# A second accumulator in PSUM for gathered expert rows, and GpSimd rows in two more stages

## The chip, the cores and the metric

The kernel runs on one NeuronCore of a Trainium2 chip. The metric is the device time of one execution in microseconds (us). The engines are named as in the profile: PE is TensorE's matrix multiply and PEld its weight load, DVE is VectorE, ACT is ScalarE, POOL is GpSimd, and SP is the engine that issues most transfers.

## The reference

One decoder layer over 512 tokens of width 1024, in float32: three token mixers in parallel (forgetting attention, windowed attention, attention to a memory), merged by gates, and then a retrieval over 16384 single-neuron experts (PEER). The change lies in the second part, after the second normalization:

```python
def peer_ffn(h, w_q, keys1, keys2, u, v):
    q = (h @ w_q).reshape(B, S, PEER_HEADS, 2, half)
    s1 = einsum('bshd,hkd->bshk', q[..., 0, :], keys1)
    s2 = einsum('bshd,hkd->bshk', q[..., 1, :], keys2)
    v1, i1 = top_k(s1, 16); v2, i2 = top_k(s2, 16)
    cand = (v1[..., :, None] + v2[..., None, :]).reshape(B, S, PEER_HEADS, 256)
    sv, si = top_k(cand, 16)
    experts = i1[si // 16] * 128 + i2[si % 16]
    gates = softmax(sv, axis=-1)
    # per token, over its 8 heads x 16 = 128 experts e:
    a = einsum('cd,ced->ce', h_c, u[e_c])
    act = gelu(a) * g_c
    out = einsum('ce,ced->cd', act, v[e_c])
```

The layer's result is the mixers' output plus `out`.

## The kernel before, in words

The 512 tokens are four blocks of 128. Block 0 goes through the mixers and the search first, blocks 1 to 3 follow together (`GROUPS`). The experts of the four blocks are then used in two ways.

**Blocks 0 and 1 gather rows.** For each of a token's 128 experts a row of `peer_u` or `peer_v` (128 tokens x 1024 numbers, 0.5 MB) is fetched by an indirect DMA, which GpSimd issues (L836). There are 512 such rows, in this order: the u rows of block 0, the v rows of block 0, the u rows of block 1, the v rows of block 1 (`JOBS`). `step()` takes the next one. It first issues gathers up to `ahead` rows in front, into a ring of five buffers (`ROWS_IN`), from the choices to near the end of spreading with two more from the `raw` buffers. Then it uses its own row. A u row is multiplied with the normalized tokens `h2n[b]` and summed along the row by one VectorE instruction (L846), which leaves one column of `acts[b]`. A v row is scaled with its column and added to the running sum `x1[b]` in SBUF by one VectorE instruction (L855). With `apart=True` a v row is instead scaled by ScalarE (L851) and added to the same sum by GpSimd (L852). After the last u row of a block, `acts[b]` goes through Gelu and is multiplied by the gates.

**Blocks 2 and 3 are dense** (`DENSE`). For each of the 128 key blocks k, `dense_u(k)` multiplies all 128 experts' u rows with the 256 tokens on PE and applies Gelu into `ga(k)`, a ring of 58 slots in the two tiles `soon` and `late`. The result is multiplied with the gates, which are zero except for chosen experts, and `dense_v(k)` multiplies it with the v rows into four PSUM banks. `dense_v` and some of `dense_u` work in pairs of rounded numbers, high part and remainder: ScalarE casts the high part, VectorE subtracts it from the original, and PE runs three products (`mm3`). A plain `dense_u` uses full float32 matmuls instead. `split_u(k)` says which form a tile takes: before, the first 57 tiles and then every second one are plain.

The stages, in order of time:

1. The mixers of block 0, then those of blocks 1 to 3, with the search and the first rows of block 0 beside them (`beside`), 190 rows in all (`EARLY_ROWS`).
2. The second search, of blocks 1 to 3, on VectorE, with `step(apart=True)` beside it and the first eight `dense_u`.
3. Choosing: `choose` for blocks 2 and 3 and `numbers_of` for block 1, on VectorE, while PE computes 24 plain `dense_u`. A row is taken for each unit of cost (`AMONG`).
4. Spreading: for 64 batches of four tokens, `build_sides` makes one-hot matrices on VectorE (L1031) and scales them on ScalarE (L1034). `spread` multiplies them on PE into a PSUM bank (L1046). VectorE multiplies part of that bank into `soon` (L1049), and ScalarE copies the rest out in three pieces (L1052), from where it goes to a DRAM buffer `gd`. 25 plain `dense_u` are laced in, and 0.8 rows for each batch (`STEPS_N`).
5. The final loop over k = 0 to 127: for each k, the gate product (L1091), the casts (L1094, L1096) and remainders (L129, L1099) of `dense_v(k+1)`, the rows that are due, the start of one `dense_u`, then PE's work of `dense_v(k)`. The rows that are left are spread evenly over the loop.

From stage 3 on, the order of instructions on PE, VectorE and GpSimd is the order of the program; ScalarE's and SP's is set by the framework's scheduler. PSUM has eight banks, which `bank(tag)` hands out: `mm` two, `tp` two, `sc` two, `tg` and `acc` one each. In spreading, `tg` holds the numbers 0 to 127 that L1031 compares with, `acc` the transposed choices, and the spread tiles alternate between `sc` and `tp`.

Of the kernel before, what the change touches and what calls it, by code (L numbers as in the profile page):

```python
# [21 lines left out]
NK = 128  # L22
# [15 lines left out]
U_SPLIT = 2  # L38
# [5 lines left out]
SPARE, STEPS_N = 4, 0.8  # L44
# [3 lines left out]
TG = 32  # L48
# [5 lines left out]
EARLY_ROWS, PER_ROW = 190, 4.6  # L54
# [3 lines left out]
def tile_block(ctx: ExitStack, tc: tile.TileContext, t: dict, out: bass.AP):  # L58
# [765 lines left out]
    known, issued, done, ahead, flying, rpool = [2 * NJ], [0], [0], [AHEAD], {}, []  # L824

    def step(apart=False):
# [16 lines left out]
        if tab == "u":  # L843
            scr = big.tile([128, D], BF16, tag="junk", name="scr")
            tc.keep_in_program_order(
                V.scalar_tensor_tensor(scr, r, 1.0, h2n[b], op0=OP.mult, op1=OP.mult, accum_out=acts[b][:, c]))  # L846
            if j == NJ - 1:
                A.activation(acts[b], acts[b], AF.Gelu)
                V.tensor_mul(acts[b], acts[b], gate[b])
        elif apart:  # L850
            A.activation(r, r, AF.Copy, scale=acts[b][:, c])  # L851
            G.tensor_tensor(x1[b], x1[b], r, op=OP.add)  # L852
        else:
            tc.keep_in_program_order(
                V.scalar_tensor_tensor(x1[b], r, acts[b][:, c], x1[b], op0=OP.mult, op1=OP.add))  # L855
# [57 lines left out]
    side[0] = iter(())  # L913
    for lb, b in enumerate(GROUPS[1]):
        x1[b] = xb[:, lb]
# [9 lines left out]
    def ga(k):  # L925
        s = k % (LAG + 1)
        return soon[:, s] if s <= LAG - GA_LATE else late[0][:, s - (LAG + 1 - GA_LATE)]
# [23 lines left out]
    def split_u(k):  # L951
        return k >= LAG and (k - LAG) % U_SPLIT > 0

    def dense_u(k):
# [4 lines left out]
        if split_u(k):  # L959
            hi, lo = (gp[0].tile([128, D], F32R, tag=tag, name=tag, bufs=1) for tag in ("uhi", "ulo"))  # L960
# [19 lines left out]
    h2f = chunks(dp.tile([128, KC, TD], F32, name="h2f", bufs=1))  # L980
# [28 lines left out]
    numbers = bank("tg")[:, :NK]  # L1009
# [3 lines left out]
    def turn_block(i):  # L1013

        ps = bank("acc")
# [21 lines left out]
    def spread(n):  # L1037
# [6 lines left out]
        ps = bank(("sc", "tp")[n % 2]).rearrange("p (t k) -> p t k", t=4)  # L1044
# [36 lines left out]
    def operands(k):  # L1081
# [6 lines left out]
        if k >= KEPT:  # L1088
            m = gq[k - k % GK][:, :, k % GK]
            g = a.rearrange("p (g t) -> p g t", t=TG)  # L1090
            V.tensor_mul(g, m, g)  # L1091
# [30 lines left out]
    credit[0] = 0.0  # L1122
# [171 lines left out]
```

## Time and profile before

| | us |
|---|---|
| median of 3 runs | 1597.82 (1595.21 to 1600.01) |
| the profiled execution | 1602.33 |
| its span, first to last instruction | 1600.5 |
| PE busy | 1532.0 |
| VectorE busy | 1404.6 |
| ScalarE busy | 788.1 |
| GpSimd busy | 798.4 |

Busy times are unions of an engine's instructions, so overlapping ones count once. A row of a group gives an instruction's line, engine, operation, output and inputs, shapes and count; behind the first bar stand the busy time in us and the mean duration of one in ns, behind the second the idle time of the engine just ahead of them and what ended it. A line of the timeline gives start, duration and instruction; `xN` merges N of them. Instructions that follow one another on an engine overlap a little, so the distance from start to start is shorter than the duration.

### The profile page before, as it was taken

To read this page: it belongs to the slowest core of one execution; us is meant where nothing else is said; L and a number is where in the kernel's file an instruction comes from. 1 tells how busy PE (TensorE), PEld (TensorE's weight loads), DVE (VectorE), ACT (ScalarE), POOL (GpSimd) and SP (SyncE) were. 2 spreads that over 40 slices of the span, in tenths; PEclk is the share of its full clock that TensorE was granted. 3 is DMA by queue.
4 is the path that set the end of the run, shared out by engine and by line. 5 is a ranking of instruction groups with operands and counts; after the bars stand their busy time and mean duration, and the time that the engine had idled before them with its cause. 6 is when DMAs were issued, how large, how long until landed. Compare 5 with 4: busy or idle time off the path is not lost.

```text
span 1600.5 us, 26571 instructions
## 1 busy us (share of the span) xinstructions
PE 1532.0 (96%) x9142; PEld 1384.7 (87%) x9142; DVE 1404.6 (88%) x2722; ACT 788.1 (49%) x1776; POOL 798.4 (50%) x624
## 2 busy tenths in 40 slices
PE   6999999999998989998898999999999999999998
PEld 5999899898897989898787999788888888888887
DVE  5677477989998999999899999888889999989997
ACT  6787426656445433454214888544444444443442
POOL 1100015776666456568764333465555565565561
PEclk9999999999998999999999999999999999999999
DMA  8586656898998799994798999999999999999995
GB/s 303 181 280 221 234 198 218 293 372 313 333 354 307 264 353 338 366 348 145 257 392 318 353 369 346 363 409 398 391 398 408 407 406 410 410 391 409 411 407 219
DMA packets 178358, 531.86 MB, mean 332 GB/s; under 512 B 17456, under 2 KB 46384, under 8 KB 178224
## 3 DMA queue, kind: packets, MB, share of 16 engines
q0 software_dynamic: 73728, 268.47, 44.7%
q1 hardware_dynamic: 94704, 226.04, 38.9%
q10 hardware_dynamic: 9792, 35.66, 5.6%
q8 instruction: 72, 1.18, 0.3%
q14 instruction: 62, 0.51, 0.1%
HBM read 515.42 MB, written 14.68 MB: 331 GB/s over the span
## 4 chain that ended last, share of the span: by engine, by line
PE 65%; DVE 12%; DMA 11%; issue 7%; ACT 3%; POOL 3%; SPq 0%; DVEq 0%; POOLq 0%; ACTq 0%
PE mm L974 16%; PE mm L144 7%; PE mm L143 7%; PE mm L145 7%; DMA row<-in_peer_v_dram,eidx 5%; DMA row<-in_peer_u_dram,eidx 4%; PE sc L144 3%; PE sc L145 3%; PE tp L143 3%; PE tp L145 3%; PE tp L144 3%; PE sc L143 3%; DVE wlo L129 2%; POOL row L836 2%; DVE mg L855 2%
## 5 line engine op out<-in xcount | busy, mean ns | idle before, releaser
L836 POOL DMA_INDIRECT row<-in_peer_v_dram,eidx x256 | 359.7, 1405 | 263.0 <-DVE mg L855 170.6
L836 POOL DMA_INDIRECT row<-in_peer_u_dram,eidx x256 | 335.0, 1308 | 271.4 <-DVE scr L846 117.6
L846 DVE SCALAR_TENSOR_TENSOR scr<-row,own 128x1024 bf16<-128x1024 f32 x256 | 312.6, 1221 | 31.6 <-DMA row<-in_peer_u_dram,eidx 29.9
L129 DVE TENSOR_TENSOR wlo<-raw,whi 128x1024 fp32r<-128x1024 f32 (+1 forms) x244 | 304.6, 1250 | 33.9 <-ACT whi L117 31.6
L855 DVE SCALAR_TENSOR_TENSOR mg<-row,acts,mg 128x1024 f32<-128x1024 f32 x237 | 304.2, 1283 | 21.0 <-DMA row<-in_peer_v_dram,eidx 18.7
L974 PE MATMUL mm<-h2f,hhi 128*128 128x256 f32 x944 | 217.4, 381 | 1.1 <-ACT late L976 1.1
L117 ACT CAST whi<-raw 128x1024 fp32r<-128x1024 f32 (+1 forms) x148 | 154.9, 1049 | 103.9 <-PE mm L144 69.9
L974 PEld LDWEIGHTS mm<-h2f,hhi 128*128 128x128 f32 x944 | 177.5, 191 | 25.7 <-ACT late L976 1.5
L190 POOL TENSOR_TENSOR rsy<-rsv,mhalf 128x4 f32<-128x4 f32 (+5 forms) x25 | 39.9, 1600 | 191.9 <-DVE rsv L189 117.6
L1094 ACT CAST ah<-ga 128x256 fp32r<-128x256 f32 x116 | 47.1, 408 | 144.3 <-PE tp L144 110.1
L143 PE MATMUL mm<-hhi,whi 128*128 128x384 f32 x320 | 111.2, 348 | 1.6 <-DVE mg L642 1.0
L145 PE MATMUL mm<-hhi,wlo 128*128 128x384 f32 x320 | 111.0, 347 | 0.0
L144 PE MATMUL mm<-hlo,whi 128*128 128x384 f32 x320 | 111.0, 347 | 0.0
L1096 ACT CAST whi<-raw 128x1024 fp32r<-128x1024 f32 x96 | 100.4, 1047 | 20.8 <-PE tp L145 9.9
L976 ACT ACTIVATE ga<-mm 128x256 f32<-128x256 f32 x84 | 32.5, 388 | 158.8 <-PE mm L974 158.5
L143 PE MATMUL sc<-whi,ah 128*128 128x512 f32 x256 | 107.2, 419 | 0.0
L143 PE MATMUL mm<-whi,hhi 128*128 128x256 f32 (+1 forms) x360 | 104.6, 292 | 1.6 <-DVE mg L642 1.0
L144 PE MATMUL mm<-wlo,hhi 128*128 128x256 f32 (+1 forms) x360 | 103.9, 289 | 2.2 <-DVE wlo L129 2.2
L145 PE MATMUL mm<-whi,hlo 128*128 128x256 f32 (+1 forms) x360 | 103.2, 288 | 0.5 <-DVE hlo L631 0.5
L144 PE MATMUL sc<-wlo,ah 128*128 128x512 f32 x256 | 101.1, 395 | 2.4 <-DVE wlo L129 2.4
L143 PE MATMUL tp<-whi,ah 128*128 128x512 f32 x256 | 101.1, 395 | 0.0
L145 PE MATMUL sc<-whi,al 128*128 128x512 f32 x256 | 101.0, 394 | 0.0
(286 smaller groups left out, 3950.3 us busy)
## 6 DMA issues: line engine op xcount, KB each, us to landing
raw<-in_peer_v_dram SPq DMA_DIRECT2D x96, 512.0 KB, 7.8
hhi<-in_uT_dram ACTq DMA_DIRECT2D x68, 512.0 KB, 7.8
raw<-in_w_tr_dram SPq DMA_DIRECT2D x48, 512.0 KB, 5.2
raw<-in_w_nat_dram SPq DMA_DIRECT2D x40, 512.0 KB, 5.9
last<-in_peer_v_dram SPq DMA_DIRECT2D x32, 512.0 KB, 7.0
hhi<-in_uT_dram SPq DMA_DIRECT2D x26, 512.0 KB, 7.1
raw<-in_w_o_dram SPq DMA_DIRECT2D x24, 512.0 KB, 5.6
gd<-st SPq DMA_DIRECT2D x24, 512.0 KB, 12.0
```

The source lines that it names most:

```text
L117: A.copy(hi[:, :n * w], raw[:, :n * w])
L129: V.tensor_sub(lo, raw, hi.bitcast(F32))
L143: PE.matmul(ps, lh, rh, start=first, stop=False)
L144: PE.matmul(ps, lh, rl, start=False, stop=False)
L145: PE.matmul(ps, ll, rh, start=False, stop=last)
L190: G.tensor_tensor(y, v, mhalf[:, :n], op=OP.pow)
L836: G.indirect_dma_start(out=r, out_offset=None, in_=t["peer_" + tab], in_offset=bass.IndirectOffsetOnAxis(ap=eidx[b][:, j:j + 1], axis=0))
L846: V.scalar_tensor_tensor(scr, r, 1.0, h2n[b], op0=OP.mult, op1=OP.mult, accum_out=acts[b][:, c]))
L855: V.scalar_tensor_tensor(x1[b], r, acts[b][:, c], x1[b], op0=OP.mult, op1=OP.add))
L974: PE.matmul(ps[:, :TD], w[:, dc], h2f[dc], start=dc == 0, stop=dc == KC - 1)
L1094: A.copy(ah, a)
L1096: A.copy(hi, raw)
```

## The change

- A tile `two` of two PSUM banks takes the place of the banks `tg` and `acc`, which are its halves in the mixers. In spreading, `numbers` and `turned` use the two `tp` banks, and the spread tiles use the two `sc` banks alone.
- After the second search (`vacant`), the v rows that VectorE takes are summed in `two`, and that sum is added to `x1[b]` after the block's last row. GpSimd's rows go on to `x1[b]` in SBUF. For the u rows of block 1, ScalarE copies `h2n[1]` to `two`, and VectorE reads it there.
- A u row can be taken apart: GpSimd multiplies it, ScalarE sums it.
- Among the choices, rows are taken in pairs on VectorE, and after every second pair one more is scaled by ScalarE. GpSimd adds it ahead of the next pair (`beside_vector`), released by a one-column copy on VectorE.
- In spreading, 0.95 rows are taken for each batch, and those with a job number divisible by four are taken apart. Before the second search 183 rows are taken, not 190.
- In the final loop the gate product is made for four k at once (in two pieces where the ring wraps from one tile to the other). All `dense_u` from the 59th on are split, with a second pair of buffers for high part and remainder in the place of `h2f`, and the last of them come one k earlier.

```diff
-U_SPLIT = 2
-SPARE, STEPS_N = 4, 0.8
+SPARE, STEPS_N = 4, 0.95
-EARLY_ROWS, PER_ROW = 190, 4.6
+EARLY_ROWS, PER_ROW = 183, 4.6
...
-    BANKS = {"mm": 2, "tg": 1, "tp": 2, "sc": 2, "acc": 1}
+    BANKS = {"mm": 2, "tp": 2, "sc": 2}
+    two = psum.tile([128, D], F32, name="two", bufs=1)
     def bank(tag):
+        if tag not in BANKS:
+            return two[:, :512] if tag == "tg" else two[:, 512:]
...
+    begun_v, scaled, vacant = set(), [], [False]
+    def beside_vector():
+        while scaled:
+            b, r = scaled.pop(0)
+            V.tensor_copy(r[:, 0:1], r[:, 0:1])
+            G.tensor_tensor(x1[b], x1[b], r, op=OP.add)
-    def step(apart=False):
+    def step(apart=False, later=False):
...
-        if tab == "u":
+        if tab == "u" and b and j == 0:
+            A.copy(two, h2n[b])
+        if tab == "u" and apart:
+            G.tensor_tensor(r, r, h2n[b], op=OP.mult)
+            A.activation(r, r, AF.Copy, accum_out=acts[b][:, c])
+        elif tab == "u":
             scr = big.tile([128, D], BF16, tag="junk", name="scr")
             tc.keep_in_program_order(
-                V.scalar_tensor_tensor(scr, r, 1.0, h2n[b], op0=OP.mult, op1=OP.mult, accum_out=acts[b][:, c]))
+                V.scalar_tensor_tensor(scr, r, 1.0, two if b else h2n[b], op0=OP.mult, op1=OP.mult,
+                                       accum_out=acts[b][:, c]))
...
+        elif apart:
+            A.activation(r, r, AF.Copy, scale=acts[b][:, c])
+            if later:
+                scaled.append((b, r))
+            else:
+                G.tensor_tensor(x1[b], x1[b], r, op=OP.add)
+        elif not vacant[0]:
...
+        elif b not in begun_v:
+            begun_v.add(b)
+            tc.keep_in_program_order(V.tensor_scalar(two, r, acts[b][:, c], None, op0=OP.mult))
+        else:
+            tc.keep_in_program_order(
+                V.scalar_tensor_tensor(two, r, acts[b][:, c], two, op0=OP.mult, op1=OP.add))
+        if j == NJ - 1:
...
+            else:
+                beside_vector()
+                V.tensor_add(x1[b], x1[b], two)
...
     def split_u(k):
-        return k >= LAG and (k - LAG) % U_SPLIT > 0
+        return k > LAG
...
-            hi, lo = (gp[0].tile([128, D], F32R, tag=tag, name=tag, bufs=1) for tag in ("uhi", "ulo"))
+            if k % 2:
+                hi, lo = (gp[0].tile([128, D], F32R, tag=tag, name=tag, bufs=1) for tag in ("uhi", "ulo"))
+            else:
+                hi, lo = halves_u[0][:, 0], halves_u[0][:, 1]
...
-    numbers = bank("tg")[:, :NK]
+    numbers = bank("tp")[:, :NK]
+    turned = bank("tp")
-        ps = bank("acc")
+        ps = turned
-        ps = bank(("sc", "tp")[n % 2]).rearrange("p (t k) -> p t k", t=4)
+        ps = bank("sc").rearrange("p (t k) -> p t k", t=4)
...
-        if k >= KEPT:
-            m = gq[k - k % GK][:, :, k % GK]
-            g = a.rearrange("p (g t) -> p g t", t=TG)
-            V.tensor_mul(g, m, g)
+        if k >= KEPT and k % GK == 0:
+            i = 0
+            while i < GK:
+                run = ga_run(k + i, GK - i)
+                n = run.shape[1]
+                g = run.rearrange("p k (g t) -> p k g t", t=TG)
+                V.tensor_mul(g, gq[k][:, :, i:i + n].rearrange("p g k t -> p k g t"), g)
+                i += n
...
-            while credit[0] >= AMONG and done[0] < known[0]:
-                credit[0] -= AMONG
+            while credit[0] >= 2.0 * AMONG and done[0] < known[0] - 3:
+                credit[0] -= 2.0 * AMONG
+                pairs += 1
+                beside_vector()
                 step()
+                step()
+                if pairs % 2:
+                    step(apart=True, later=True)
+    beside_vector()
...
-            step()
+            step(apart=done[0] % 4 == 0)
...
-        while k_u < min(NK, LAG + (NK - LAG) * (k + 1) // (NK - 5)):
+        while k_u < min(NK, LAG + (NK - LAG) * (k + 1) // (NK - 6)):
```

More of the change, by code (lines that the diff above doesn't have):

```diff
@@ L842, in step @@
         r, c = flying.pop(n), slice(j, j + 1)
-        if tab == "u":
+        if tab == "u" and b and j == 0:
[4 more added lines that the diff above has]
+        elif tab == "u":
             scr = big.tile([128, D], BF16, tag="junk", name="scr")
             tc.keep_in_program_order(
-                V.scalar_tensor_tensor(scr, r, 1.0, h2n[b], op0=OP.mult, op1=OP.mult, accum_out=acts[b][:, c]))
-            if j == NJ - 1:
+                V.scalar_tensor_tensor(scr, r, 1.0, two if b else h2n[b], op0=OP.mult, op1=OP.mult,
[8 more added lines that the diff above has]
+            tc.keep_in_program_order(
+                V.scalar_tensor_tensor(x1[b], r, acts[b][:, c], x1[b], op0=OP.mult, op1=OP.add))
+        elif b not in begun_v:
+            begun_v.add(b)
+            tc.keep_in_program_order(V.tensor_scalar(two, r, acts[b][:, c], None, op0=OP.mult))
+        else:
+            tc.keep_in_program_order(
+                V.scalar_tensor_tensor(two, r, acts[b][:, c], two, op0=OP.mult, op1=OP.add))
+        if j == NJ - 1:
+            if tab == "u":
                 A.activation(acts[b], acts[b], AF.Gelu)
                 V.tensor_mul(acts[b], acts[b], gate[b])
[L850 to L855, printed above, removed]
+            else:
+                beside_vector()
+                V.tensor_add(x1[b], x1[b], two)
     def beside():
@@ L925, in ga, with ga_run @@
     def ga(k):
-        s = k % (LAG + 1)
-        return soon[:, s] if s <= LAG - GA_LATE else late[0][:, s - (LAG + 1 - GA_LATE)]
+        return ga_run(k, 1)[:, 0]
+    def ga_run(k, n):
+        s, edge = k % (LAG + 1), LAG + 1 - GA_LATE
+        return soon[:, s:min(s + n, edge)] if s < edge else late[0][:, s - edge:min(s - edge + n, GA_LATE)]
     def fetch_u(k):
@@ L979, in tile_block @@
     h2T = [chunks(x) for x in pair(BIG)]
-    h2f = chunks(dp.tile([128, KC, TD], F32, name="h2f", bufs=1))
+    h2f = chunks(dp.tile([128, KC, TD], F32, tag="h2f", name="h2f", bufs=1))
+    halves_u = []
     k_u, share[0] = 0, 0.0
@@ L1121, in tile_block @@
     ahead[0] = AHEAD + MORE
-    credit[0] = 0.0
+    credit[0], pairs = 0.0, 0
     for job in (*(choose(cp, f, lb, iota_k, chosen[DENSE[lb - 1]]) for lb in (1, 2)), numbers_of(cp, f, 0, 1, iota_k)):
@@ L1177, in tile_block @@
         split(h2s[0][dc], h2s[1][dc], h2f[dc])
+    halves_u.append(dp.tile([128, 2, D], F32R, tag="h2f", name="u2", bufs=1))
     begun = []
@@ L1185, in tile_block @@
         begun = []
-        while k_u < min(NK, LAG + (NK - LAG) * (k + 1) // (NK - 5)):
-            assert not begun and not (split_u(k_u) and any(split_u(n) for _, n in us))
+        while k_u < min(NK, LAG + (NK - LAG) * (k + 1) // (NK - 6)):
+            assert not begun
             begun.append((dense_u(k_u), k_u))
             next(begun[-1][0])
-            if split_u(k_u):
-                next(begun[-1][0])
+            next(begun[-1][0])
             k_u += 1
```

2 lines of the change are left out of this document (added).

## The prediction

> **What bounds the kernel now.** I read the page first, then busy time by stage, then the groups, the waits and the timeline of the longest stage.
>
> ```profile
> span 1600.5 us, 26571 instructions
> PE 1532.0 (96%) x9142; PEld 1384.7 (87%) x9142; DVE 1404.6 (88%) x2722; ACT 788.1 (49%) x1776; POOL 798.4 (50%) x624
> ```
>
> The profiled execution took 1602.3 us, 4.5 above the median of 1597.8; the sum below is made on its span and its difference laid on the median. At 96% and 88%, PE and VectorE must be compared stage by stage:
>
> ```profile
> core 0: us, PE busy (x) PEld busy (x) DVE busy (x) ACT busy (x) POOL busy (x), PEclk, DMA share, GB/s
> 550.00:692.00 142.00, 131.32 (x836) 127.91 (x835) 134.19 (x214) 54.51 (x97) 81.54 (x67) 0.95 0.97 356
> 692.00:778.00 86.00, 78.77 (x421) 73.72 (x420) 81.20 (x507) 39.79 (x58) 70.62 (x63) 0.96 0.65 225
> 778.00:862.00 84.00, 77.68 (x361) 67.82 (x359) 80.38 (x128) 12.74 (x30) 54.05 (x41) 1.00 0.95 359
> 862.00:1016.00 154.00, 150.66 (x934) 138.72 (x935) 147.96 (x224) 128.61 (x488) 50.66 (x50) 0.98 0.97 343
> 1016.00:1600.00 584.00, 576.99 (x2934) 494.74 (x2932) 528.76 (x701) 233.53 (x357) 325.99 (x211) 1.00 0.99 390
> ```
>
> The stages are: end of the mixers and start of the second search; the rest of that search; choosing; spreading; the final loop over 128 key blocks. The reader is to see four different limits. In the search VectorE leads. In choosing and spreading both engines are within 7 us of the stage. In the final loop PE is busy for 577 of 584 us and VectorE is idle for 55. DMA is almost saturated there too (share 0.99).
>
> **The change, part by part.** Rows are 512 jobs. Before: 190 by the end of the mixers, 19 during the search, 36 among the choices (their costs sum to 36.1), 51 in spreading (64 x 0.8), so 216 in the final loop. After: 183, 19, 45 (18 pairs of VectorE rows, with a GpSimd row behind every other pair), 60 (64 x 0.95, of which 15 have a job number divisible by four and go to ScalarE and GpSimd), so 205 in the final loop. VectorE loses 7, 0, 6 and 11 rows in these places.
>
> *Fewer early rows.*
>
> ```profile
> 550.00:692.00 142.00, 74.60 (x58) 0.95 0.97 356
> 699.01 3.70 DVE L129 TENSOR_TENSOR wlo<-raw,whi 128x1024 fp32r<-128x1024 f32 x1
> L129 DVE TENSOR_TENSOR wlo<-raw,whi 128x1024 fp32r<-128x1024 f32 x95 | 115.9, 1220 | 1.8 <-ACT whi L1096 1.8
> L852 POOL TENSOR_TENSOR mg<-mg,row 128x1024 f32<-128x1024 f32 x19 | 45.2, 2379 | 0.3
> L836 POOL DMA_INDIRECT row<-in_peer_v_dram,eidx x256 | 359.7, 1405 | 263.0 <-DVE mg L855 170.6 <-issue 20.5 <-DVE scr L846 16.9
> ```
>
> The first row is the v rows of L855 alone: 58 in 74.6 us, 1.29 each, up to the point where the first GpSimd rows begin. VectorE is the fuller engine on both sides of it, so 7 x 1.29 = 9.0 us go from the path. The 19 GpSimd rows begin that much earlier, so they don't hold the end. The chain may pass through row transfers at places, so I take -8, between -10 and 0.
>
> *Choosing.* VectorE keeps 36 rows. Nine tiny copies are added, nine GpSimd adds of 2.38 us and nine ScalarE scalings (ScalarE is busy for 13 of 84). A split on VectorE beside such adds took 3.70 us instead of its usual 1.22, so an add that is late for the two sheltered rows can hold up a later operation with two SBUF inputs. Ends: 0, and 9 x 2.4 = 21 us. With VectorE at 80.4 of 84 some slack exists, and two rows of 1.28 cover an add that starts in time; I take +2, near the sheltered end. Each add waits for the tiny copy, and the next gathers' descriptors are queued on POOL behind it. POOL goes from 54 to 54 + 9 x 2.38 + 9 x 1.41 = 88 us if descriptors stay as long as they are, so it is full, and rows may come late; that is the unsheltered end.
>
> *Spreading.*
>
> ```profile
> L1034 ACT ACTIVATE o<-o,eT 128x128 f32<-128x128 f32 x256 | 81.6, 393 | 20.4 <-DVE o L1031 20.3
> L851 ACT ACTIVATE row<-row,acts 128x1024 f32<-128x1024 f32 x19 | 21.6, 1150 | 23.6 <-DMA row<-in_peer_v_dram,eidx 23.6
> 921.05 1.05 PE L1046 MATMUL sc<-o 128*128 128x128 f32 x8
> 923.72 0.60 ACT L1052 COPY st<-sc 128x128 f32<-128x128 f32 x3
> 925.76 1.05 PE L1046 MATMUL sc<-o 128*128 128x128 f32 x8
> ```
>
> PE keeps all its work (150.7 of 154), so VectorE's six fewer rows give nothing. ScalarE takes 15 x 1.15 + about 1 for the copy of the normalized rows into PSUM: 128.6 + 18 = 147. The spread tiles have two banks instead of four, so the bank written at 921.05 must be free at 925.76; ScalarE lets go of it at 924.32, a margin of 1.4 us that one 1.15 us row nearly eats. An in-order ScalarE that waits for a GpSimd product also delays PE. Ends: -2 (PE's gaps) and +10 (each of the 15 rows holding PE for some 0.7 us); I take +2, since the margin covers one row.
>
> *Final loop, PE.* 35 plain u tiles become split tiles. The first row here is a stretch in the middle of the loop, in the columns of the stages.
>
> ```profile
> 1300.00:1400.00 100.00, 100.00 (x521) 86.39 (x520) 94.43 (x112) 40.96 (x64) 59.55 (x39) 1.00 1.03 410
> 1039.75 3.45 PE mm L974 x16
> 1301.66 0.28 PE L143 MATMUL mm<-hlo,uhi 128*128 128x256 f32 x1
> 1304.48 0.40 PE L143 MATMUL sc<-whi,ah 128*128 128x512 f32 x1
> ```
>
> A plain tile occupies PE for 3.45 us; a split one, from its first matmul to the next tile's, 2.82. 35 x 0.63 = 22 us less: PE needs 555.
>
> *Final loop, VectorE.*
>
> ```profile
> L855 DVE SCALAR_TENSOR_TENSOR mg<-row,acts,mg 128x1024 f32<-128x1024 f32 x128 | 164.1, 1282 | 15.1 <-DMA row<-in_peer_v_dram,eidx 13.7
> L846 DVE SCALAR_TENSOR_TENSOR scr<-row,own 128x1024 bf16<-128x1024 f32 x88 | 107.6, 1222 | 10.0 <-DMA row<-in_peer_u_dram,eidx 8.9
> L963 DVE TENSOR_TENSOR ulo<-hhi,uhi 128x1024 fp32r<-128x1024 f32 x35 | 42.7, 1220 | 0.0
> 1429.15 1.22 DVE L963 TENSOR_TENSOR ulo<-hhi,uhi 128x1024 fp32r<-128x1024 f32 x1
> 1430.28 1.22 DVE L129 TENSOR_TENSOR wlo<-last,whi 128x1024 fp32r<-128x1024 f32 x1
> 1431.42 0.42 DVE L1099 TENSOR_TENSOR al<-ga,ah 128x256 fp32r<-128x256 f32 x1
> 1431.75 0.42 DVE L1091 TENSOR_TENSOR ga<-gq,ga 128x256 f32<-128x256 f32 x1
> 1432.09 2.60 DVE L855 SCALAR_TENSOR_TENSOR mg<-row,acts,mg 128x1024 f32<-128x1024 f32 x2
> ```
>
> From start to start a split's remainder takes 1.13 and a gate product 0.34. 35 more remainders cost +39.6. The 96 gate products (32.6) become 22 of four blocks and 4 of two, where the ring of 58 slots wraps: 22 x 1.13 + 4 x 0.60 (between 0.34 and 1.13 by size) = 27.3, so -5.3. Eleven fewer u rows: -13.4. One more add of the PSUM sum: +1.2. VectorE needs 528.8 + 22.1 = 551. ScalarE gets 35 casts more on 234 of 584 us; they are hidden by its idle time. The gathers lose 11 of 0.5 MB, about 6 of the 228 MB that 390 GB/s make in 584 us, so DMA at the 410 GB/s of the stretch 1300 to 1400 would need 541.
>
> ```profile
> DVE al L1099 <- ACT ah L1094: 17.6, 16, 3.2
> DVE mg L855 <- DMA row<-in_peer_v_dram,eidx: 13.7, 19, 2.1
> DVE scr L846 <- DMA row<-in_peer_u_dram,eidx: 8.9, 9, 2.2
> DVE wlo L129 <- ACT whi L1096: 5.6, 7, 1.6
> ```
>
> So PE (555) and VectorE (551) become equal bounds. VectorE's waits for ScalarE (17.6 + 5.6) come from a ScalarE that follows PE, and should mostly go as PE gets slack; of the 22.6 for row transfers I keep some 17, and 5 for the ends. 551 + 22 = 573, that is -11. Ends: 559 (555 and PE's own gaps of 4) and 606 (VectorE with all its idle time, 551 + 55).
>
> *PSUM as operand.* A row now reads and writes PSUM on VectorE.
>
> ```profile
> L1031 DVE TENSOR_TENSOR o<-tg,eT 128x1024 f32<-128x1024 f32 x64 | 77.7, 1217 | 0.0
> L1010 DVE COPY tg<-cst x1: 292/292/292, 511.6 to 511.6; 128x128 f32<-128x128 f32 x1
> L778 DVE CAST p<-pos 128x128 f32<-128x128 uint32 x3 | 0.7, 220 | 0.0
> ```
>
> Reading PSUM costs nothing: L1031 takes 1217 ns beside 1220 for L963 in SBUF. For writing there is one copy, 292 ns, beside 220 for a cast within SBUF. Ends: 0 and +72 ns a row. I take 0, since the in-place sum is nearer to L1031 in kind and size.
>
> [...]
>
> **Sum.** -8 + 2 + 2 - 11 = -15: span 1585.5, its execution 1587.3, median 1582.8.
>
> **The rivals.**
> - *VectorE becomes the bound and keeps its waits* (slower). In the final loop its 551 plus idle time sets the end. With all 55 the loop takes 606, +22, and the kernel is at +18, 1616; with 45, 1606. It decides once more than 37 us of idle time stay (551 + 37 = 588, which uses up the 4 us net gain elsewhere). For it: the row waits are the transfers' and DMA stays nearly full. Against: in the stretch 1300 to 1400 VectorE was 94% busy though PE set the pace, and in spreading 96%. Chance 0.17.
> - *Writing PSUM is dearer.* 72 ns on 205 rows is +14.8 in the final loop, and about +3 on the 36 + 45 before it: 1601. For it only the small copy, against it L1031. [...] Chance 0.10.
> - *Spreading pays for two banks and a full ScalarE*: +10 instead of +2, 1591. Chance 0.10.
> - *The early rows weren't on the path*: 0 instead of -8, 1591. Against it are the 134 busy of 142 us. Chance 0.09.
>
> **How the numbers follow.** The forecast has 0.54, with 1572 to 1592 as its own range. The low end of the whole range is all good ends but the choices': -10 + 2 - 2 - 25 would be 1563; as they hardly come together I stop at 1568. The high end is the first rival with 45 us of idle time and a little more, 1608. What a measurement tells from no change is 0.3%, 4.8 us. Faster: 0.54, and some 0.11 from the two rivals that end at 1591: 0.65. Slower: 0.17, and 0.03 from the PSUM price: 0.20. Same: 0.15.
>
> **What would show it.** After: the first GpSimd rows of the search some 9 us earlier; GpSimd adds in the choices beside VectorE rows at 1.28, with no split or comparison far above its usual time; the spread stage within 152 to 158 us and ScalarE above 90% of it; in the final loop 70 remainders, no plain tile but one, PE near 97% and VectorE near 96%, the wait for `ah` below 8 us. I would be wrong if rows in PSUM took 1.35, if PE stood idle in the final loop for VectorE by more than 30 us, or if POOL's adds made rows late in the choices.

## The result, and the profile after

The changed kernel takes 1615.2 us (median of six executions, 1606.8 to 1619.6) against 1598.2 for the kernel before on the same chip: a ratio of 1.0092, with a 95% interval of 1.0072 to 1.0112. On another chip it was 1612.8 against 1601.7, 1.0085 (1.0062 to 1.0107). The forecast was 1583: wrong in sign, by 32 us.

The profiled execution of the changed kernel took 1606.8 us, the shortest of its six. The first fence has the busy line of its page, the second its busy time by stage, in the columns that the prediction showed (PE, PE's weight loads, VectorE, ScalarE, GpSimd, granted clock, DMA share, GB/s). The five stretches run up to its own landmarks: the mixers of blocks 1 to 3, the rest of the second search, choosing, spreading, the final loop.

```profile
PE 1514.0 (94%) x9422; PEld 1374.8 (86%) x9422; DVE 1428.6 (89%) x2661; ACT 843.1 (53%) x1849; POOL 800.2 (50%) x648
```

```profile
427.00:655.00 228.00, 211.69 (x1344) 195.62 (x1343) 210.83 (x326) 99.07 (x219) 135.70 (x105) 0.96 0.91 325
655.00:781.00 126.00, 110.67 (x631) 105.84 (x632) 115.21 (x568) 58.71 (x90) 84.55 (x74) 0.93 0.66 235
781.00:880.00 99.00, 90.07 (x409) 78.00 (x407) 89.35 (x175) 22.39 (x40) 67.27 (x54) 0.98 0.88 334
880.00:1034.00 154.00, 148.91 (x926) 136.32 (x927) 141.97 (x215) 138.88 (x515) 93.78 (x77) 0.98 1.01 368
1034.00:1600.00 566.00, 558.19 (x3220) 488.13 (x3219) 548.32 (x645) 269.19 (x394) 271.79 (x200) 1.00 1.00 393
```

And the same kind of answer for the kernel before, at the landmarks that it has for the first three of these stretches:

```profile
427.00:645.00 218.00, 204.66 (x1320) 193.09 (x1318) 201.50 (x314) 95.33 (x205) 126.62 (x98) 0.96 0.91 325
645.00:773.00 128.00, 118.26 (x657) 112.92 (x657) 122.85 (x596) 59.10 (x93) 90.64 (x83) 0.95 0.77 281
773.00:862.00 89.00, 82.68 (x384) 72.22 (x382) 84.11 (x153) 13.16 (x30) 58.60 (x45) 1.00 0.93 347
```

Both kernels reach 427 us together. Then the mixers take 228 instead of 218 us and choosing 99 instead of 89; the rest of the search, which should have become 9 us shorter, takes 126 instead of 128, with PE busy for only 110.7 of them. Spreading is nearly as before. Only the final loop gains: 14 us by the landmarks below (the stretches of 584 and 566 both end at 1600, and so hold different tails behind the loop). So the losses in the mixers and the search, which the prediction had costed at nothing, and in choosing, which it had costed at 2, swallow the gain.

To compare kernels I use four landmarks, each the start of the first or last of a group of instructions: the last candidate sum on GpSimd (the search ends), the first comparison for the spread tiles (choosing ends), the first remainder `al` (spreading ends), the last `al<-ga` (end of the loop). These are the groups in the changed kernel:

```profile
L693 POOL TENSOR_TENSOR cand<-v x64: 201/228/1318, 201.2 to 780.9; 128x24 f32<-128x24 f32 x16, 128x16 f32<-128x16 f32 x16, 128x48 f32<-128x48 f32 x16, 128x8 f32<-128x8 f32 x8
L1069 DVE TENSOR_TENSOR o<-tp,eT x64: 1206/1214/1218, 880.7 to 1021.7; 128x1024 f32<-128x1024 f32 x64
L1142 DVE TENSOR_TENSOR al<-ga,ah x116: 409/417/427, 1033.9 to 1595.8; 128x256 fp32r<-128x256 f32 x116
```

This gives 780.9 for the end of the search, then 99.8 for choosing, 153.2 for spreading and 561.9 for the loop. All profiles by these landmarks, in us, with the ratio of the times to the kernel before on the same chip:

| kernel | search ends | choosing | spreading | loop | ratio (95%) |
|---|---|---|---|---|---|
| before | 773.2 | 89.3 | 152.7 | 575.9 | 1 |
| changed | 780.9 | 99.8 | 153.2 | 561.9 | 1.0092 (1.0072 to 1.0112) |
| changed, again | 781.1 | 98.2 | 154.0 | 563.3 | 1.0085 (1.0062 to 1.0107) |
| early183 | 761.8 | 90.1 | 148.4 | 581.4 | 0.9959 (0.9943 to 0.9974) |
| final_only | 768.6 | 89.2 | 153.1 | 571.6 | 0.9968 (0.9954 to 0.9982) |
| two_tile | 783.5 | 89.9 | 152.0 | 579.2 | 1.0093 (1.0078 to 1.0107) |
| two_tp | 772.9 | 89.9 | 150.4 | 580.3 | 1.0056 (1.0036 to 1.0075) |
| tp_only | 770.8 | 89.9 | 148.4 | 579.5 | 1.0008 (0.9991 to 1.0026) |
| sep_banks | 762.6 | 100.4 | 160.3 | 563.2 | 0.9933 (0.9919 to 0.9946) |
| sep_again | 764.8 | 97.8 | 154.7 | 563.1 | 0.9944 (0.9924 to 0.9963) |
| sep_nochoose | 760.8 | 91.0 | 155.7 | 575.2 | 0.9984 (0.9970 to 0.9999) |
| sep_noadd | 765.0 | 95.7 | 158.4 | 563.3 | 0.9935 (0.9910 to 0.9961) |
| sep_third | 763.5 | 103.1 | 155.0 | 563.1 | 0.9987 (0.9972 to 1.0003) |
| sep_spread | 756.6 | 98.4 | 152.3 | 574.3 | 0.9986 (0.9974 to 0.9997) |
| sep_more3 | 769.3 | 99.0 | 154.4 | 570.8 | 0.9961 (0.9942 to 0.9980) |
| after_tp | 768.3 | 99.2 | 160.9 | 560.9 | 0.9984 (0.9971 to 0.9997) |

Executions of one kernel differ by a few us in where the search ends (the seven profiles whose names begin with sep_ share the code of that part: 756.6 to 769.3), so one profile's landmark there counts for some 6 us either way. The boundary between spreading and the loop moves too: before, early183, tp_only and final_only share the code of spreading, and it takes 148.4 to 153.1. So the ratios decide.

### The profile page after: what moved, and what is told of

Read it like the earlier page. It is cut to its first block, busy times and chain, and to the rows that moved or that the text cites. A ratio compares the mean times of both kernels' runs of the same rounds, so it can differ in the third digit from the quotient of the medians.

```text
span 1605.0 us, 27116 instructions
## 1 busy us (share of the span) xinstructions
PE 1514.0 (94%) x9422; PEld 1374.8 (86%) x9422; DVE 1428.6 (89%) x2661; ACT 843.1 (53%) x1849; POOL 800.2 (50%) x648
## 4 chain that ended last, share of the span: by engine, by line
PE 58%; DVE 14%; issue 11%; DMA 7%; POOL 6%; ACT 3%; SPq 0%; POOLq 0%; DVEq 0%; ACTq 0%
PE mm L146 9%; PE mm L145 9%; PE mm L147 9%; PE mm L1010 5%; POOL row L846 5%; DMA row<-in_peer_v_dram,eidx 3%; PE sc L1084 3%; DVE wlo L131 3%; PE sc L146 2%; PE sc L147 2%; PE tp L146 2%; PE tp L145 2%; PE sc L145 2%; PE tp L147 2%; DVE two L877 2%
## 5 line engine op out<-in xcount | busy, mean ns | idle before, releaser
L846 POOL DMA_INDIRECT row<-in_peer_v_dram,eidx x256 | 323.4, 1263 | 276.6 <-DVE two L877 148.8
L846 POOL DMA_INDIRECT row<-in_peer_u_dram,eidx x256 | 313.4, 1224 | 239.3 <-DVE scr L861 134.6
L131 DVE TENSOR_TENSOR wlo<-raw,whi 128x1024 fp32r<-128x1024 f32 (+1 forms) x244 | 313.4, 1285 | 38.7 <-ACT whi L119 34.1
L877 DVE SCALAR_TENSOR_TENSOR two<-row,acts,two 128x1024 f32<-128x1024 f32 x169 | 217.0, 1284 | 6.1 <-DMA row<-in_peer_v_dram,eidx 3.8
L119 ACT CAST whi<-raw 128x1024 fp32r<-128x1024 f32 (+1 forms) x148 | 155.0, 1049 | 112.8 <-PE mm L146 65.3
L861 DVE SCALAR_TENSOR_TENSOR scr<-row,own 128x1024 bf16<-128x1024 f32 x128 | 156.5, 1222 | 19.9 <-DMA row<-in_peer_u_dram,eidx 19.1
L861 DVE SCALAR_TENSOR_TENSOR scr<-row,two 128x1024 bf16<-128x1024 f32 x115 | 139.5, 1213 | 2.2 <-DMA row<-in_peer_u_dram,eidx 1.3
L145 PE MATMUL sc<-whi,ah 128*128 128x512 f32 x256 | 100.8, 394 | 0.0
L146 PE MATMUL tp<-wlo,ah 128*128 128x512 f32 x256 | 100.6, 393 | 0.0
L147 PE MATMUL tp<-whi,al 128*128 128x512 f32 x256 | 100.2, 391 | 0.0
```

What stands on the lines that cost most here:

```text
L119: A.copy(hi[:, :n * w], raw[:, :n * w])
L131: V.tensor_sub(lo, raw, hi.bitcast(F32))
L145: PE.matmul(ps, lh, rh, start=first, stop=False)
L146: PE.matmul(ps, lh, rl, start=False, stop=False)
L147: PE.matmul(ps, ll, rh, start=False, stop=last)
L846: G.indirect_dma_start(out=r, out_offset=None, in_=t["peer_" + tab], in_offset=bass.IndirectOffsetOnAxis(ap=eidx[b][:, j:j + 1], axis=0))
```

## The experiments

**One part at a time, on both sides.** Theory one: the tile of two banks, which replaces the separate banks `tg` and `acc` already in the mixers, costs the 8.5 us there. Theory two: the seven early rows fewer do it. Theory three: the granted clock.

early183 is one constant of the kernel before:

```
-EARLY_ROWS, PER_ROW = 190, 4.6
+EARLY_ROWS, PER_ROW = 183, 4.6
```

> The kernel before with 183 instead of 190 rows among the mixers and nothing else; the seven rows go to later stages. The prediction's step says 8 us less up to the end of the second search, of which the final loop gives back at most 9 (seven rows of 1.28): 1590 to 1599, with the last rows of that stretch some 8 us earlier. Theory one (the shared tile of the two PSUM banks costs the mixers 8.5 us, and the seven rows were never on the path): mixers and search as before, 1598 to 1602. Theory two (the seven rows fewer are themselves what shifted the mixers and lengthened them): the mixers of blocks 1 to 3 end 8 to 9 us later, 1606.

1594.2 against 1601.0. The search ends at 761.8, against 773.2, 768.6 and 770.8 in the three profiles with 190 rows and separate banks (before, final_only, tp_only): about 9 us earlier, as the prediction's step said. The loop gets longer by 5.5, but spreading is 4.3 shorter; together they take 1.2 more. Theory two falls.

two_tile takes only the bank layout:

```
-    BANKS = {"mm": 2, "tg": 1, "tp": 2, "sc": 2, "acc": 1}
+    BANKS = {"mm": 2, "tp": 2, "sc": 2}
+    two = psum.tile([128, D], F32, name="two", bufs=1)
     def bank(tag):
+        if tag not in BANKS:
+            return two[:, :512] if tag == "tg" else two[:, 512:]
...
-    numbers = bank("tg")[:, :NK]
+    numbers = bank("tp")[:, :NK]
+    turned = bank("tp")
...
-        ps = bank(("sc", "tp")[n % 2])...
+        ps = bank("sc")...
```

> The kernel before with the two banks tg and acc made halves of one PSUM tile, the spread tiles in two banks instead of four and the table of key numbers moved; rows, choices and final loop as before. Theory one (the shared tile makes the mixers wait): mixers of blocks 1 to 3 end some 8.5 us later and spreading pays about 2, 1607 to 1610, and the order of instructions there is that of the changed kernel. Theory two (the number of early rows) and theory three (a lower granted clock by chance): mixers as before, 1598 to 1602.

1615.8: theory one, and more than it asked for. This part alone makes the kernel as slow as the whole change does. The search ends 10 to 15 us later, while spreading with two banks instead of four takes 152.0 instead of 152.7 us.

The timeline of PE shows what changes. First the kernel before, where the window attention's last block runs (line 354 transposes the probabilities, 513 accumulates in `acc`, 347 transposes the next heads' queries through `tg`):

```profile
500.21 0.49 PE L347 MATMUL tg<-cst,qn 128*128 128x128 f32 x3
500.53 1.00 PE L513 MATMUL acc<-sv,pT 128*128 128x64 f32 x8
...
505.57 1.97 PE L513 MATMUL acc<-sv,pT 128*128 128x64 f32 x8 [0.68 <-ACT pT L356]
509.25 1.65 PE L347 MATMUL tg<-cst,qn 128*128 128x128 f32 x3 [1.71 <-ACT qn L333]
```

The same work in two_tile, where `tg` and `acc` are halves of `two` (lines 350 and 516, the division on VectorE is line 374):

```profile
518.60 1.97 PE L516 MATMUL two<-sv,pT 128*128 128x64 f32 x8 [0.73 <-ACT pT L359]
523.41 1.12 PE L378 MATMUL tp<-cst,o 128*128 128x128 f32 x4 [2.83 <-DVE o L374]
524.32 0.85 PE L350 MATMUL two<-cst,qn 128*128 128x128 f32 x3
...
526.24 0.84 PE L350 MATMUL two<-cst,qn 128*128 128x128 f32 x3
```

In the kernel before a transpose into `tg` stands among the accumulations, and PE has other work while a block is finished. With the shared tile there is no transpose into the first half until the accumulators in the second are complete and divided, and PE stands idle for 2.83 us until that division (`o`) ends. The whole trace bears this out: 108 matmuls write `tg` or, in its place, the first half of `two`. In the kernel before 20 of them lie between the first accumulation of a block and its division (19 in sep_banks, below), in two_tile and in the changed kernel none. So the program's order of instructions itself is another one: what uses the two halves has been put one after the other.

The 2.83 us are only a part of the loss. From 427.5 us, where the forgetting attention's branch ends, to the first sum of the mixers' output at 611.6, the kernel before takes 184.1 us, with PE busy for 172.2; two_tile takes 194.8, from 428.6 to 623.4, with PE busy for 180.2. So 2.7 of these 10.7 us are idle time of PE, and 8.0 are work: 28 more matmuls lie in this stretch, where the window attention has been pushed back.

**The banks separated again.** sep_banks is the changed kernel with the two banks in a PSUM pool of their own, closed after the mixers:

```
-    two = psum.tile([128, D], F32, name="two", bufs=1)
+    mixing = ExitStack()
+    pair_of = mixing.enter_context(tc.tile_pool(name="mixing", bufs=1, space=PSUM))
     # tg and acc are tiles of pair_of
...
     pre.close()
+    mixing.close()
+    two = ctx.enter_context(tc.tile_pool(name="sum", bufs=1, space=PSUM)).tile([128, D], F32, ...)
```

> The changed kernel, but tg and acc are two tiles of a PSUM pool of their own, closed after the mixers; the two-bank sum is allocated from the freed banks afterwards. Theory one: the 8.5 us of the mixers come back, 1607, with the choices as slow as in the changed kernel (91 us). Theory two or three: 1615, mixers ending as late as in the changed kernel.

1590.8 against 1601.0: 24 us less than the changed kernel, three times what theory one asked for, and faster than the kernel before. Theories two and three, which asked for 1615, fall. The search ends at 762.6 instead of 781; choosing stays at 100.

Of these 18 us, 11 lie in the mixers, which end at 643.5 instead of 654.6. The other 7 lie in the rest of the search, and there the changed kernel has one wait that no other has. The fence shows ScalarE and, in its last row, PE in the changed kernel:

```profile
722.96 1.15 ACT L864 ACTIVATE row<-row,acts 128x1024 f32<-128x1024 f32 x1 [4.18 <-DMA row<-in_peer_v_dram,eidx]
731.23 1.15 ACT L864 ACTIVATE row<-row,acts 128x1024 f32<-128x1024 f32 x1 [6.48 <-DMA row<-in_peer_v_dram,eidx]
739.53 1.15 ACT L864 ACTIVATE row<-row,acts 128x1024 f32<-128x1024 f32 x1 [7.16 <-DMA row<-in_peer_v_dram,eidx]
741.52 0.47 ACT L721 COPY qp<-mm 128x384 f32<-128x384 f32 x1
742.04 1.65 PE L725 MATMUL sc<-keys,qp 128*128 128x128 f32 x6 [13.10 <-ACT qp L721]
```

ScalarE scales three rows for GpSimd, each of which it has to wait for, ahead of a copy (`qp`) that PE needs. PE stands for 13.1 us. In the other three profiles of the changed kernel this wait is 12.6, 12.7 and 12.9 us; in every other kernel, sep_banks included, the longest wait for such a copy is 2.4 to 6.9. So in the changed kernel the shared tile costs more than in two_tile because it also comes with another order in the search. Why the scheduler chose it wasn't traced.

The kernel with separate banks was timed once more on another chip:

> The kernel with separate mixer banks once more, on another chip and with more executions: 0.990 to 0.995 of the kernel before if the first comparison holds (1590.8 against 1601.0).

1591.4 against 1599.8, ratio 0.9944: it holds. This is the version that beats both kernels.

**What in the shared tile costs.** two_tp is two_tile, tp_only the kernel before, after_tp the changed kernel, each with this edit; in tp_only nothing is shared and `tg` stands unused in the mixers:

```
-            ps = bank(("tg", "tp")[n % 2])      # heads' transposes
+            ps = bank("tp")
```

> The kernel before with the shared tile of two banks, but the heads' transposes use the two tp banks alone, so that in the mixers nothing but the accumulators of attention stands in the shared tile (its second half). Theory one (a transpose into one half waits for the accumulators in the other): mixers of blocks 1 to 3 end as in the kernel before or within 3 us, 1600 to 1604. If it isn't the two halves but the tile's place or kind that costs: as with the shared tile, 1613 to 1616.

> The kernel before, in which the heads' transposes use the two tp banks alone; tg stands unused in the mixers, the accumulators keep a bank of their own, nothing is shared. If the 7 us that remained with the shared tile and transposes in tp alone come from the transposes having one bank less, this kernel is as slow, mixers of blocks 1 to 3 ending 6 to 8 us late: 1603 to 1606. If they come from accumulators in the shared tile, it is as the kernel before: 1597 to 1600.

> The changed kernel, with the shared tile kept, but the heads' transposes in the two tp banks alone. If it is transposes and accumulators in the two halves of one tile that wait for each other, the search ends some 10 us earlier than in the changed kernel (781) and the whole takes 1600 to 1605. If the tile itself costs, whatever is written into it, 1611 to 1616.

two_tp took 1604.9 (1.0056) and after_tp 1596.8 (0.9984): with the heads' transposes out of the shared tile, 0.4% of the 0.9% come back in the kernel before, and 1.0% of the some 1.5% (1.0092 or 1.0085 against 0.9933 or 0.9944) in the changed one. tp_only took 1602.5 against 1601.7: a bank less for the transposes costs nothing that can be measured, though the mixers end 6 us later, since the rest of the search is that much shorter. So most of the loss is the meeting of transposes and accumulators in one tile; after_tp gets back more than was expected of it (1600 to 1605). Some 0.4 to 0.5% remain in two_tp and after_tp, with nothing but accumulators in the shared tile during attention; their profiles show no single place for it, and it stays open.

**The final loop alone.** final_only is the kernel before with all u tiles after the ring split, the halves in the place of `h2f`, merged gate products and u one block earlier (that part of the diff, unchanged).

> The kernel before with the changed final loop alone: all u tiles after the ring are split, halves in the place of h2f, gate products for four blocks at once, u tiles done one block earlier. 216 rows stay in the loop instead of 205, summed in SBUF. The prediction's step: VectorE 551 + 11 x 1.28 = 565 busy. If VectorE's work and its 21 us of idle time set the end, the loop takes 585 and the kernel is as before, 1595 to 1600. If PE sets it (558 busy), the loop takes 570 as in the changed kernel: 1583. Mixers, search, choices and spreading as before under either.

1595.9 against 1601.0; by the landmarks the loop goes from 575.9 to 571.6 with 216 rows, and is 561.9 in the changed kernel with 205. That is nearer to the first case (no change) than to the second (562 by the landmarks). Here is the loop's busy time in final_only:

```profile
1011.00:1583.00 572.00, 555.97 (x3202) 485.15 (x3201) 559.29 (x664) 268.35 (x395) 354.31 (x211) 1.00 1.01 397
```

The next two fences have the same for the changed kernel's first profile, and for another of its profiles (after_l3), in which TensorE was granted 0.95 of its clock through the whole loop:

```profile
1034.00:1596.00 562.00, 554.19 (x3202) 484.86 (x3201) 547.11 (x643) 269.19 (x394) 271.79 (x200) 1.00 1.00 396
```

```profile
1044.00:1606.00 562.00, 553.40 (x3198) 483.83 (x3197) 546.76 (x641) 268.65 (x393) 272.53 (x200) 0.95 1.00 396
```

Between final_only and the changed kernel eleven rows leave the loop. PE's work stays (3202 matmuls, 556 and 554 us), VectorE's falls by 12.2 us, and the loop by 9.7. Nine rows make 10.7 us of VectorE's work and 12.1 of the loop between sep_nochoose and sep_again. So with 214 or 216 rows the loop follows VectorE's work. With 205 rows PE has 8 us of idle time and VectorE 15: they are nearly equal bounds, as the prediction said, and nothing here shows which of them ends the loop.

The lower clock doesn't tell either, though PE is busy for 554 and 553 us and the loop takes 561.9 and 563.1. The next four rows are two pairs, the first profile ahead of after_l3 in each: one group of matmuls of the loop, with the shortest, median and longest duration in ns, and eight matmuls of a plain u tile in spreading.

```profile
L145 PE MATMUL tp<-whi,ah x252: 389/390/404, 1036.6 to 1594.7; 128*128 128x512 f32 x126
L145 PE MATMUL tp<-whi,ah x252: 389/390/404, 1046.4 to 1605.5; 128*128 128x512 f32 x126
902.91 1.89 PE L1010 MATMUL mm<-h2f,hlo 128*128 128x256 f32 x8
910.12 1.96 PE L1010 MATMUL mm<-h2f,hlo 128*128 128x256 f32 x8
```

The plain matmuls follow the clock: they start 216 ns apart at 1.00 and 224 at 0.95. Those of the loop don't: they start 230 to 232 ns apart (over 512 columns, median) and 119 (over 256) at either clock. What paces PE's matmuls in the loop isn't shown, and that PE keeps its pace is no sign that it had room.

The row transfers are a rival that wasn't tested. The DMA share is 1.00 in the loop, and by an estimate nine rows of 0.5 MB are 12 us at its 395 GB/s. VectorE waits for rows for 8.5 us in sep_nochoose and 7.1 in final_only, against 1.3 in the changed kernel, so they may have a part.

**Choosing.** Three edits on the kernel with separate banks. sep_nochoose puts back the rows of the kernel before (36, all on VectorE, one at a time); sep_noadd drops the nine GpSimd adds; sep_third gives their rows to VectorE:

```
 sep_nochoose: while credit[0] >= AMONG and done[0] < known[0]: credit[0] -= AMONG; step()
 sep_noadd:    beside_vector() without G.tensor_tensor(x1[b], x1[b], r, op=OP.add)
 sep_third:    step() in place of step(apart=True, later=True)
```

> The kernel with separate mixer banks, and among the choices the rows of the kernel before: single rows, all 36 on VectorE, no GpSimd add, no tiny copy. Nine rows move to the final loop. Theory one (VectorE's waits for late rows 5, the tiny copies 2 and the splits and comparisons that run slower beside the adds 2.5 make the choices 10 us longer): the choices take 90 instead of 100 us; the final loop gets nine rows of 1.28 more on VectorE, of which up to 11 may show: 1582 to 1592. Theory two (the choices are longer because of their place behind the faster search): 100 us again, 1595 or above.

> The kernel with separate mixer banks, with GpSimd's nine adds among the choices left out (their rows are gathered, scaled and touched by the tiny copy, but do not reach the sum, so the output lacks them). If the adds themselves cost (contention with VectorE's two-input operations, and POOL's time before the next gathers), the choices fall from 100 us by most of 10: 90 to 93. If gathering and scaling on ScalarE in program order make rows late, 97 to 100 stay.

> The kernel with separate mixer banks, with the nine rows that GpSimd adds among the choices given to VectorE. VectorE gets nine rows of 1.28 (11.5) and loses nine tiny copies (1.3) and the contention (2.5). If giving those rows to GpSimd saved VectorE time, the choices take 108 to 112 us here against 100. If GpSimd's help costs as much as it saves, 98 to 102.

Choosing takes 91.0 with 36 rows on VectorE, 103.1 with 45 there (+12.1), and 97.8 to 100.4 with nine of the 45 on GpSimd (sep_banks, sep_again, sep_spread, sep_more3; mean 98.9). So the help of GpSimd saves 4 us of 12 and costs 8; sep_third lies between its two cases, nearer to the second. sep_noadd lies between its own: without the adds 95.7 remain, so the adds themselves cost some 3, and 4.7 come with the gathering, the scaling on ScalarE and the tiny copies. The groups of VectorE in choosing, in the changed kernel:

```profile
L877 DVE SCALAR_TENSOR_TENSOR two<-row,acts,two 128x1024 f32<-128x1024 f32 x35 | 45.0, 1285 | 4.3 <-DMA row<-in_peer_v_dram,eidx 3.8
L803 DVE TENSOR_TENSOR hot<-hot,idb 128x2048 bf16<-128x2048 bf16 x6 | 8.5, 1413 | 0.0
L806 DVE TENSOR_TENSOR hot<-hot 128x1024 bf16<-128x1024 bf16 x6 | 5.4, 893 | 0.1
L833 DVE COPY row<-row 128x1 f32<-128x1 f32 x9 | 1.3, 147 | 1.2 <-ACT row L864 1.2
```

and the first three of these in the kernel without the adds, sep_noadd:

```profile
L876 DVE SCALAR_TENSOR_TENSOR two<-row,acts,two 128x1024 f32<-128x1024 f32 x35 | 45.1, 1288 | 4.4 <-DMA row<-in_peer_v_dram,eidx 3.8
...
L803 DVE TENSOR_TENSOR hot<-hot,idb 128x2048 bf16<-128x2048 bf16 x6 | 7.3, 1219 | 0.0
L806 DVE TENSOR_TENSOR hot<-hot 128x1024 bf16<-128x1024 bf16 x6 | 4.1, 690 | 0.1
```

The adds lengthen the products (L803) and sums (L806) of the one-hot matrices, which read SBUF twice (1413 against 1219 ns, 893 against 690: 1.2 + 1.2 us), and leave the rows alone, which read their sum in PSUM (1285 and 1288 ns; none of the 169 in the changed kernel takes more than 1291). What a row with its sum in SBUF would lose beside an add, no run shows. The sheltering with two PSUM rows, on which the part rests, works while an add runs beside them, but the add of 2.36 us begins only after the tiny copy, and its end meets the next product or sum. The tiny copies take 1.3 and 1.2 of waiting for ScalarE. The rows' 3.8 us of waiting for transfers are there with and without adds, and not in sep_nochoose and sep_third (0.4 and 1.0 us of idle time ahead of the rows), where ScalarE scales no row. Choosing's waits in the changed kernel say where these come from:

```profile
ACT row L864 <- DMA row<-in_peer_v_dram,eidx: 15.4, 4, 7.5
POOL row L846 <- DVE two L874: 13.2, 1, 13.2
POOL row L846 <- issue: 8.5, 29, 0.6
PEld mm L1010 <- ACT ga L1012: 4.4, 3, 2.9
DVE two L877 <- DMA row<-in_peer_v_dram,eidx: 3.8, 6, 0.9
PE mm L1010 <- ACT ga L1012: 3.4, 2, 2.5
```

ScalarE, in program order, waits for the rows that it is to scale (15.4 us) and its next activation then holds PE (4.4 and 3.4). GpSimd's first gather of the stage waits 13.2 us for a buffer that the first row frees. sep_more3 tries a third lent buffer (`MORE` 3 instead of 2):

> The kernel with separate mixer banks, with one more row buffer lent to the gathers in the choices and in spreading (three instead of two), so that gathers run one row further ahead. If VectorE's and ScalarE's waits for row transfers (5 us on VectorE) are what lengthens the choices besides the adds, they take 95 to 97 instead of 100: 1586 to 1589. If POOL's own queue of descriptors and adds sets when rows arrive, nothing changes: 1589 to 1593.

Choosing stays at 99.0: buffers aren't what is short there. Its ratio, 0.9961, is no better than that of sep_banks; the loop took 570.8 in its profile, 7 us more than elsewhere, in the longest of its twelve executions (1604.6). VectorE waits there once for 7.1 us for a cast of ScalarE, which waits 9.3 us for its v tile (at most 4.8 in the other kernels with the new loop); whether the third lent buffer made that tile late wasn't tested.

For the whole kernel the nine rows still pay: sep_nochoose has theory one's choosing, but takes 1596.1 and not 1582 to 1592 (0.9984 against 0.9933 and 0.9944), since nine rows cost 12 us in the loop and 8 in choosing. And sep_third (0.9987) is 7 to 9 us behind sep_banks and sep_again, more than the 4 that its choosing shows; its profile has no place for the rest.

**Spreading.** sep_spread takes spreading's rows back to those of the kernel before (51 instead of 60, none on ScalarE and GpSimd).

> The kernel with separate mixer banks, with spreading's rows as in the kernel before: 51, all on VectorE, none on ScalarE and GpSimd. Nine more rows go to the final loop, 1.33 us each as the kernel without GpSimd rows in the choices showed: +12 there. If the rows on ScalarE cost spreading little (the prediction's +2), spreading takes 152 to 154 us instead of about 155 and the whole is 1598 to 1602. If they hold up PE by 6 or more (the stall of that profile), the loss and the gain nearly cancel: 1593 to 1597.

Spreading takes 152.3 instead of 154.7 (sep_again), the loop 574.3 instead of 563.1; 1598.6, as by the first of the two cases. In sep_banks and after_tp spreading took 160 and 161, in sep_noadd 158. The timelines of ScalarE and of PE in sep_banks, in this order, show one stall of 6 us at its end:

```profile
1010.35 1.04 ACT L1141 CAST whi<-raw 128x1024 fp32r<-128x1024 f32 x1 [4.75 <-DMA gd<-st]
1011.61 0.59 ACT L1092 COPY st<-sc 128x128 f32<-128x128 f32 x3
```

```profile
1012.25 2.07 PE L1086 MATMUL sc<-o 128*128 128x128 f32 x8 [6.23 <-ACT st L1092]
1016.41 1.05 PE L1086 MATMUL sc<-o 128*128 128x128 f32 x8
```

ScalarE's order is the only one of the big engines' that isn't written by hand in this stretch, and it has the final loop's first cast of a v tile ahead of the last evictions. The cast waits 4.75 us for its tile, behind the gates' transfer; the spread banks stay full and PE stands. after_tp has two such stalls, of 2.56 and 3.16 us, and sep_noadd one of 2.31; sep_again, the same kernel as sep_banks, has none above 1.4 us. Over the whole stage PE waits for these evictions for 2.2 to 7.6 us in the kernels with rows on ScalarE (0.5 in after_l3), and for 0.9 in sep_spread and 0.3 in two_tile, which have none there. The eight matmuls after the stall of sep_banks take 2.07 us, the next eight 1.05, and the granted clock is 0.71 from 1005 to 1015 us and 0.93 from 1015 to 1023.3, by an estimate from these two 0.50 from some 1009.3 to 1016.1. So this stall costs a little more than its length.

**The executions that no profile had shown.** The changed kernel was profiled again (after_again), to see whether the executions near the median lose their 8 us in one place. But the first two profiles of it were each the shortest of six. Two more:

> The changed kernel, one more look. If the profiled execution is near 1614 instead of 1607, the stage that is longer than in the first profile (search to 781, choices 99, spreading 153, from there to the end 570) holds the 7 us.

> The changed kernel, one more look, for the same comparison of its stages with the first profile (781, 99, 153, 570).

after_l4 took 1611.0: search to 783.1, choosing 100.2, spreading 152.9, loop 563.7; of the 4 us over the first profile 2.2 lie before the end of the search and 1.8 in the loop. after_l3 took 1617.7 at a granted clock of 0.93 over the whole run: 788.6, 98.3, 156.6, 563.1, that is 7.7 of its 11 us before the end of the search; as it ran at another clock, it says little of the others. So no stage holds after_l4's 4 us alone, and the rest of the 8 us up to the median is in no profile: it stays open. The changed kernel's mean clocks (0.972 to 0.978 in both comparisons, against 0.982 to 0.987 in sep_banks) fit its idle gaps of PE: in the first profile the granted clock is 0.50 from 732.1 to 745.7 us, where PE waits for its 13.1 us in the search. That all of the difference in clock comes from such gaps was not tested.

## Why the prediction was wrong, point by point

- **Missing term: the mixers and the search.** The prediction costed the bank layout for the spread tiles alone ("the spread tiles have two banks instead of four") and for the reads and writes of VectorE. The edit changes `bank()` for every stage, and the mixers' transposes and accumulators were put into halves of one tile. The term measures +15 on the kernel before (two_tile), and 22 to 25 in the changed kernel (1.4 to 1.6%, from 0.9944 and 0.9933 against 1.0085 and 1.0092). In the changed kernel's profiles 11 us of it lie in the mixers, whose order became another, and 7 in the search, where PE waits for ScalarE for 13 us (at most 6.9 in the other kernels); the rest has no place in these profiles. None of the rivals had the term. This is the step that turned the sign.
- **Early rows, -8 (-10 to 0): right.** The search ends some 9 us earlier in early183. In the changed kernel the losses in the mixers and the search hide it. That the seven rows come back in the loop was in the loop's term; in early183 spreading and loop together are only 1.2 longer.
- **Choosing, +2 (0 to 21): mis-sized.** It is +8 (98.9 against 91.0) to +10 (99.8 against 89.3). The prediction held to the sheltered end. That an add doesn't slow two rows with their sum in PSUM was not shown by the kernel before; in the changed kernel it holds (1285 ns, 1288 without the adds). But a part of the products and sums isn't sheltered (2.4 us), the tiny copies cost 2.5 with their waits, rows come late by 3.8, and ScalarE's waiting reaches PE (3.4 us). What would show it wrong ("if POOL's adds made rows late") came in part: rows are late, but in sep_noadd too. GpSimd, which the prediction had full at 88 us, was busy for 67 of 99.
- **Spreading, +2 (-2 to +10): right within its ends,** 0 to +4 in most profiles against 152.7 of before and 152.3 of sep_spread, +6 to +8 in three (sep_banks, after_tp, sep_noadd). Two banks by themselves cost nothing (152.0 in two_tile), and ScalarE was 139 busy of 154. The longest stalls come from ScalarE's order at the end of the stage; the rows on ScalarE add to PE's waits (0.9 us without them, 2.2 to 7.6 with them in all profiles but one).
- **Final loop, -11 (559 to 606 for 584): right.** By the landmarks 575.9 became 561.9, 563.3 and 563.7: -12 to -14 (the old loop with 216 rows took 579.2 to 580.3 in three other kernels, by which it would be more). The waits for `ah` fell from 17.6 to 1.8, below the 8 asked for, there are 70 remainders (two groups of 35), and VectorE is 97% busy: 548.3 of 566, where the sum had 551 and 22 of idle time. Groups of VectorE in the loop of the changed kernel, and the row of that wait:

```profile
L877 DVE SCALAR_TENSOR_TENSOR two<-row,acts,two 128x1024 f32<-128x1024 f32 x127 | 163.1, 1284 | 1.8
L999 DVE TENSOR_TENSOR u<-hhi,u 128x1024 fp32r<-128x1024 f32 x35 | 42.6, 1218 | 1.8 <-issue 1.8
L1133 DVE TENSOR_TENSOR ga<-gq,ga 128x1024 f32<-128x1024 f32 x20 | 24.3, 1217 | 0.0
```

```profile
DVE al L1142 <- ACT ah L1137: 1.8, 4, 0.6
```

- **PSUM as operand, 0 (0 to +72 ns a row): right.** A v row takes 1284 ns with the sum in PSUM, 1282 in SBUF, and a u row of the loop 1215 with the tokens in PSUM, 1222 in SBUF, so neither reading nor writing PSUM adds anything to these rows. The price of the rival was too high as it stood: of the loop's 205 rows only the 128 v rows write PSUM, and 72 ns on these are 9.2 us, not 14.8.
- **Rivals.** The first named 1606 to 1616, which the kernel takes, but by luck: VectorE does come to lead the loop together with PE, but its idle time is 18 us in the last stretch and not 45 to 55, and the kernel loses nothing there. The other three didn't happen as told.

Without the missing term the steps close: -9 (early rows) + 9 (choosing) + 2 (spreading) - 13 (loop) = -11, and the kernel with separate banks measures -10.2 and -8.5.

## What to carry to other kernels

When buffers are merged so that a later stage gets a bigger one, cost the stages that used them separately, first of all those long before the change: list every user of the name, not only the lines that the diff touches. Two halves of one tile need not overlap as two tiles do (20 transposes among the accumulations in two tiles here, none in halves of one), and the loss can be one of order, that shows as work pushed back and idle time of the leading engine and not as a longer instruction. A pool that ends where the stage ends gives both. And help from an idle engine is worth what the bound engine sheds after its copies, waits and slower neighbours: here, by the length of choosing, 4 of 12 us.

## What the hardware showed that I had not expected

- A granted clock of 0.95 instead of 1.00 slowed the matmuls of the plain u tiles (224 instead of 216 ns from start to start) and not those of the final loop (230 to 232 and 119 ns at both), which took 563 and 562 us.
- GpSimd's adds of 2.36 us lengthened only some products and sums in choosing, by up to 0.7 us (in the changed kernel 1.80 instead of 1.22 for one product, 1.35 instead of 0.69 for one sum), and no row with its sum in PSUM.
- The eight matmuls after a stall of 6.2 us on PE took 2.07 us, about twice the 1.05 of the next eight of their group.
